# A two-layer encoder trunk on eight cores: the FFN down projection by seven block products, with residuals kept in DRAM

## The chip, the cores and the metric

The kernel runs on all 8 NeuronCores of one Trainium2 chip. Each core works on its own 2048 tokens; there is no traffic between cores. The metric is the device time of the slowest core, in microseconds (us). Cores 0 to 3 are one die, cores 4 to 7 the other.

Some executions of every version, the kernel before included, fall into a slower state: the cores of one die, sometimes of both, or a pair of cores, show a lower granted TensorE clock in the records, and the time is longer. Each such run is named below as slow or disturbed, and no difference is explained by one. Where a run of the kernel itself is compared, fast runs are compared with fast runs, and where single cores are compared, undisturbed cores with undisturbed cores.

## The reference, cut to what matters

```python
def swiglu(n, w_gate, w_up, w_down):
    return (jax.nn.silu(n @ w_gate) * (n @ w_up)) @ w_down

h = x                                   # (2, 8192, 1024) float32
for i in range(2):
    h = h + mixer_i(rms_norm(h))        # layer 0: convolutions, layer 1: chunked gating
    h = h + memory_cross_attention(rms_norm(h), mem)
    h = h + swiglu(rms_norm(h), w_gate[i], w_up[i], w_down[i])   # d_ff = 2816
return rms_norm(h)
```

## The kernel before

A core holds its tokens as four tiles of 512. `hT` is the float32 residual of the four tiles, kept in on-chip memory for the whole run (in the profile `hT_67` to `hT_70` are tiles 0 to 3); `nT` (`nT_71` to `nT_74`) is the normed input of a block in fp16. A Python scheduler lays out the five instruction streams ahead of time: it takes operations in program order, may look a few operations ahead on each engine (`AHEAD`), and picks by deadlines taken from its own cost model. So the order of each stream is fixed before the kernel runs, and an operation that waits holds back all that stands behind it in its stream.

Some words: a *slab* is a block of weights that one DMA loads; the *root* is the reciprocal root of a norm (`rs` in the traces), and the *scalings* multiply by it; a down phase without the seven products is called *plain*.

The FFN treats two token tiles at a time, a "pair"; the first pair is tiles 0 and 1, the second is tiles 2 and 3. It cuts d_ff into two runs of 12 and 10 blocks of 128. In each run there is a gate phase and then a down phase. The gate phase already uses seven block products instead of eight for a 2x2 block product (two feature blocks by two token tiles, with the contraction cut in two); the weight sums and input differences that this needs are made on VectorE. The down phase is plain:

```python
FPARTS = (12, 10)
AHEAD = {"pe": 6, "act": 32, "dve": 32, "pool": 1, "sp": 1}
...
for part, nf in enumerate(FPARTS):
    ...                                             # gate phase: seven products per unit
    for m in range(KC):                             # down phase: 8 output blocks
        w = self.wc(f"fd{part}", l, m)
        for ti, tt in enumerate(tts):
            rk = (lambda k, ti=ti: self.hid[ti][:, k, :])
            if part == 0:
                b = self.linear(w, nf, rk, self.hid_s[ti][0:nf], TT)
                # hT[tt][m] += ps[b]   (one addition on DVE)
                continue
            self.out_block(w, m, tt, nf, rk, self.hid_s[ti][0:nf], jobs[ti], 1)
            if m == KC - 1:
                if final:
                    self.push_store(tt, jobs[ti])
                else:
                    self.push_finish(jobs[ti], 5)
```

In the last layer the final norm works in place on `hT`, and the result is stored from there. This is pushed onto a queue of side work that is issued little by little while matmuls run:

```python
def push_store(self, tt, j, c0=0, n=TT, hs=None):
    def pair(k):
        j.scale(k)                                  # DVE: hT[k] *= gain * rstd, in place
        j.scale(k + 1)
        self.P.dma("sp", nm, hs[k:k + 2], (), out=self.out[tt, :, k:k + 2, c0:c0 + n],
                   in_=self.hT[tt][:, k:k + 2, c0:c0 + n])
    self.push(j.key, j.rstd, 5)
    for k in range(0, KC, 2):
        self.push(j.key, lambda k=k: pair(k), 5)
```

The start loads the input tiles one after the other behind the first weight slabs:

```python
self.load_x(0, "a", (), ("act", "sp"))
sl = [self.slab("ev_in", 0, c)[1] for c in (0, 4, 8, 16)]
self.load_x(1, "a", [sl[1]])                        # tile 1 behind the second weight slab
self.load_x(2, "a", [self.hT_s[1][4]])
self.load_x(3, "a", [self.hT_s[2][4]])
```

The softmax here doesn't subtract the row's maximum and nothing guards it: scores larger than these inputs give would overflow.

Of the kernel before, what the change touches and what calls it, by code (L numbers as in the profile page):

```python
# [14 lines left out]
KC = 8  # L15
# [9 lines left out]
FMAX = max(FPARTS)  # L25
KH = KC // 2
# [65 lines left out]
class Prog:  # L92
    ENGS = ("pe", "act", "dve", "pool", "sp")
    AHEAD = {"pe": 6, "act": 32, "dve": 32, "pool": 1, "sp": 1}
# [5 lines left out]
    DMA_RATE = 320e3  # L100
    EPOCH = 500
# [16 lines left out]
    def dma_part(self, eng, sem, slot, first, reads=(), **kw):  # L118
        prev = slot.w
        o = self.add(eng, lambda e: e.dma_start(**kw), reads, [slot] if first else [], dma=sem, cost=kw["in_"].nbytes())  # L120
        if not first:
            assert prev.dma == sem
            slot.w = o
        return o
# [47 lines left out]
    def schedule(self):  # L172
# [4 lines left out]
        link = 0.0  # L177
# [128 lines left out]
WCOLS = {"fgu": 512, "od_v": 512, "xo": 512}  # L306
# [9 lines left out]
class Builder:  # L316
    def __init__(self):
# [11 lines left out]
        self.wcache = {}  # L329
        self._declare_dram()  # L330
# [34 lines left out]
    def _declare_dram(self):  # L365
        nc = self.nc

        def din(name, shape):
# [9 lines left out]
                  for n, L, K, C in WSHAPES}  # L378
        self.out = nc.dram_tensor("out", [NT, 128, KC, TT], F32, kind="ExternalOutput").ap()

    def _alloc(self):
# [92 lines left out]
        sw_lo = tw_lo - 3 * KH * 2 * 128 * 2  # L474
        self.off = sw_lo
        self.sw, self.sw_s = self.tiles("sw", [128, 3, KH, 2, 128], FP16, 3)
        self.off = sw_lo - 2 * FMAX * TT * 2
        self.hid, self.hid_s = [], []
        for t in range(2):
            a, b = self.tiles(f"hid{t}", [128, FMAX, TT], FP16, FMAX)  # L480
            self.hid.append(a)
            self.hid_s.append(b)
        self.off = self.ends["ff"] = sw_lo - 2 * FMAX * TT * 2 - 6 * TT * 4
# [147 lines left out]
    def ld(self, name, layer, c0, at=None, after=()):  # L631
# [10 lines left out]
        self.wn += 1  # L642
        flat = self.nc.alloc_sbuf_tensor_at(f"wbuf{i}", [128, kc * cw], FP16, offset=lo)
# [5 lines left out]
        return flat[:, :].rearrange("p (k c) -> p k c", c=cw), sl  # L649

# [99 lines left out]
    def first_norms(self):  # L750
        js = [self.main_job(t, V_GMIX, pre=False, split=True) for t in range(NT)]
# [4 lines left out]
        for j, lag in ((js[0], 0), (js[1], 4), (jh, 8), (js[2], 10), (js[3], 18)):  # L756
# [42 lines left out]
    def l0_mixer(self):  # L799
# [19 lines left out]
        order = [(0, TT), (1, TT), (-1, H2), (2, TT), (3, TT)]  # L819
# [3 lines left out]
        def by_chunk():  # L823
# [3 lines left out]
            for q in range(2):  # L827
                for k in range(KC):
                    def fn(e, k=k, q=q):
                        for b, w in list(zip(bs, ws))[2 * q:2 * q + 2]:  # L830
                            ins = e.matmul(self.ps[b][:, :], lhsT=w[0](k), rhs=self.nT[0][:, k, :], start=(k == 0),
                                           stop=(k == KC - 1))
                        return ins
                    P.add("pe", fn, reads=[ws[2 * q][1][0], self.nT_s[0][k]],
                          writes=[self.ps_s[b] for b in bs[2 * q:2 * q + 2]], cost=2 * _mm_cost(TT))
                    self.tick(0.25)
            for b in bs:
                self.reserved.discard(b)
            first.update(zip(cs, bs))

        def side_a(tt, n, j):
            rk, rs = rhs_of(tt)
            if tt == 0 and j < 2:
                bv, bg = first[j], first[4 + j]
# [51 lines left out]
        def gated(tt, half):  # L896
            if tt in (2, 3):
                gate_b(tt - 1, half)
            elif tt < 0:
                gate_b(0, half)  # L900
        rhs_of(0)
        by_chunk()
        for tt, n in order:
            for j in range(2):
# [128 lines left out]
    def l1_mixer(self):  # L1033
# [10 lines left out]
        for fh in range(2):  # L1044
            self.slab("od_v", 0, 4 * fh, self.kv_lo if fh else None)
# [99 lines left out]
    def xattn(self, l):  # L1145
# [40 lines left out]
        def out(tt, m):  # L1186
            self.out_block(((lambda k: self.VW[:, k, m * 128:(m + 1) * 128]), self.VW_s), m, tt, KC,
                           lambda k: pt(tt, k)[0], [pt(tt, k)[1] for k in range(8)], jobs[tt], 3)
            if m == KC - 1:
# [42 lines left out]
    def weight_sums(self, slab, ss, s21):  # L1232
        w = slab.rearrange("p k (g j c) -> p k g j c", g=2, j=2)
        a11, a12, a21, a22 = w[:, 0:KH, :, 0, :], w[:, KH:KC, :, 0, :], w[:, 0:KH, :, 1, :], w[:, KH:KC, :, 1, :]
# [4 lines left out]
        return [lambda: tt(t[:, 0], a21, a22, ALU.add, ts[0], [ss, s21]),  # L1239
# [325 lines left out]
```

## Time and profile before

| | before |
|---|---|
| time, median of 3 runs | 1618.05 us (1617.05 to 1618.2) |
| spans of the eight cores, profiled run | 1608.9 to 1616.7 us |
| TensorE (PE) busy | 1581.7 us, 98% |
| VectorE (DVE) busy | 1035.0 us, 64% |
| moved by DMA | 130.66 MB |

This is the head of the profile page of the kernel before, with the row of TensorE from its 40-slice table (a digit is the busy share of a slice in tenths) and its chain of waits, by engine:

```profile
PE 1581.7 (98%) x7930; PEld 759.5 (47%) x7930; DVE 1035.0 (64%) x1662; ACT 710.0 (44%) x1174; POOL 71.5 (4%) x150
...
PE   6999999999999999999999999999999999999998
...
PE 94%; DMA 3%; ACT 1%; issue 1%; DVE 1%; POOL 0%; DVEq 0%; ACTq 0%; POOLq 0%; SPq 0%
```

The kernel is bound by TensorE everywhere but in the first slice and at the very end. The chain of work that ended last, near the end of the kernel, shows a down phase of run 0, with the plain start of the gate phase behind it, as one piece of 208 matmuls (start, length, what):

```profile
1469.89 44.89 PE ps L624 x208
```

That is 215.8 ns for a matmul of 512 columns. The Trainium skill, "TensorE: Matmul & The Clock Gate", § Back-to-back issue gap, gives N/2.4 + 2.5 ns warm, which is 215.8 ns for N = 512; here the trace agrees to the digit (that section calls it the gap of an isolated matmul; see the last section). So a **loss** can be computed for any stage of the kernel: its length less the sum of N/2.4 + 2.5 ns over its matmuls. The stage ledger in this document was made that way, from the matmul records of the trace. Its stages run from the first matmul of one to the first of the next.

These are three stretches of core 5, the slowest one before: the two kinds of down phase, then the last layer's first gate phase of the second pair. The columns are busy us of the engines with the number of instructions, the granted clock, the busy share of the 16 DMA engines, and GB/s:

```profile
508.50:549.90 41.40, 41.40 (x193) 18.74 (x192) 14.17 (x22) 0.63 (x1) 1.06 (x2) 1.00 0.37 70
611.10:645.60 34.50, 34.50 (x161) 15.68 (x160) 22.70 (x39) 10.07 (x16) 0.68 (x2) 1.00 0.43 81
1395.90:1469.70 73.80, 73.49 (x341) 33.19 (x340) 55.35 (x85) 47.68 (x72) 4.23 (x8) 1.00 0.68 147
```

On core 5, the slowest one before, a down phase of run 0 (508.50 to 549.90 us) is 192 matmuls in 41.40 us, one of run 1 (611.10 to 645.60 us) 160 in 34.50 us, with PE busy all the time. The gate phase has 340 matmuls in 73.80 us, while DVE is busy 55 of the 74 us.

### The profile page before, as it was taken

What the parts mean: (1) busy time and instruction counts of PE and PEld (TensorE: products, weight loads), DVE (VectorE), ACT (ScalarE), POOL (GpSimd) and SP (SyncE); (2) the same over time, 40 slices, a digit from 0 to 9 for tenths busy, and PEclk for the clock granted to TensorE, in tenths of its full rate; (3) what the DMA queues carried; (4) which work ended last, traced back from release to release, by engine and by line L of the source; (5) the groups of instructions that cost most, each with busy time, mean ns of one, the idle gap of its engine ahead of it and who ended that gap; (6) DMA issues with size and microseconds to landing.
All of it is one profiled execution on the core that took longest, in us unless ns stands there. A gap on an engine that the chain in (4) does not pass through costs nothing.

```text
span 1616.7 us, 24172 instructions; the slowest of 8 cores (1608.9 to 1616.7 us)
## 1 busy us (share of the span) xinstructions
PE 1581.7 (98%) x7930; PEld 759.5 (47%) x7930; DVE 1035.0 (64%) x1662; ACT 710.0 (44%) x1174; POOL 71.5 (4%) x150
## 2 busy tenths in 40 slices
PE   6999999999999999999999999999999999999998
PEld 2444674444444444444444455544444444444445
DVE  3777575656895466773656864755788357684456
ACT  2523475455462143740536533455555134371243
POOL 1000010000000000000000000000000000000000
PEclk9999999999999999999999999999999999999999
DMA  8344269310245263453453155130065344475342
GB/s 197 86 92 80 40 108 220 79 27 1 53 79 95 48 110 74 92 92 73 75 96 64 27 80 91 21 58 1 0 110 105 72 78 92 79 155 118 69 90 105
DMA packets 31193, 130.66 MB, mean 81 GB/s; under 512 B 3680, under 2 KB 8160, under 8 KB 24544
## 3 DMA queue, kind: packets, MB, share of 16 engines
q0 software_dynamic: 18720, 100.03, 35.1%
q1 hardware_dynamic: 12064, 28.04, 5.8%
q8 instruction: 67, 1.10, 0.3%
q10 hardware_dynamic: 288, 1.05, 0.2%
q14 instruction: 54, 0.44, 0.1%
HBM read 216.51 MB, written 8.39 MB: 139 GB/s over the span
## 4 chain that ended last, share of the span: by engine, by line
PE 94%; DMA 3%; ACT 1%; issue 1%; DVE 1%; POOL 0%; DVEq 0%; ACTq 0%; POOLq 0%; SPq 0%
PE ps L624 66%; PE ps L622 23%; PE ps L110 2%; PE ps L783 1%; PE ps L1137 1%; DMA wbuf_113<-w_ev_in 1%; DMA hT_68<-x_in 1%; DMA wbuf_131<-w_ev_out 0%; PE ps L1082 0%; DMA wbuf_192<-w_od_out 0%; DMA wbuf_199<-w_xqT 0%; ACT yst L110 0%; ACT L110 0%; ACT t_3_66 L110 0%; DVE pT L110 0%
## 5 line engine op out<-in xcount | busy, mean ns | idle before, releaser
L110 ACT ACTIVATE ps<-ps 128x512 f32<-128x512 f32 x88 | 50.9, 581 | 198.2 <-PE ps L624 197.7
L624 PE MATMUL ps<-pT,VW 128*128 128x512 f16 x512 | 118.7, 379 | 2.5 <-DVE pT L110 2.5
L110 DVE TENSOR_TENSOR hT_67<-hT_67,ps 128x512 f32<-128x512 f32 x64 | 44.0, 687 | 69.1 <-PE ps L624 66.7
L622 PE MATMUL ps<-tw,sw 128*128 128x512 f16 x352 | 83.5, 379 | 0.0
L624 PE MATMUL ps<-tw,sw 128*128 128x512 f16 x352 | 83.3, 379 | 0.0
L624 PEld LDWEIGHTS ps<-pT,VW 128*128 128x128 f16 x512 | 49.9, 98 | 63.4 <-issue 3.4
L110 ACT ACT_TABLE_LOAD x50 | 64.2, 1283 | 32.4 <-DMA hT_67<-x_in 9.3
L110 DVE TENSOR_TENSOR hT_68<-hT_68,ps 128x512 f32<-128x512 f32 x64 | 43.9, 686 | 47.0 <-PE ps L624 46.9
L110 DVE TENSOR_TENSOR hT_69<-hT_69,ps 128x512 f32<-128x512 f32 x64 | 43.9, 686 | 46.4 <-PE ps L624 46.1
L110 DVE TENSOR_TENSOR hT_70<-hT_70,ps 128x512 f32<-128x512 f32 (+1 forms) x72 | 44.9, 627 | 43.4 <-PE ps L624 39.2
L110 ACT ACTIVATE pT<-ps,epsc 128x512 f16<-128x512 f32 x64 | 43.7, 683 | 27.0 <-PE ps L624 25.8
L624 PEld LDWEIGHTS ps<-tw,sw 128*128 128x128 f16 x352 | 34.5, 98 | 41.5
L622 PEld LDWEIGHTS ps<-tw,sw 128*128 128x128 f16 x352 | 34.5, 98 | 41.5
L110 ACT ACTIVATE t_2_65<-ps 128x512 f32<-128x512 f32 (+1 forms) x53 | 30.8, 581 | 48.9 <-PE ps L624 33.0
L110 ACT ACTIVATE t_0_63<-ps 128x512 f32<-128x512 f32 (+1 forms) x56 | 32.2, 574 | 35.8 <-PE ps L624 23.2
L622 PE MATMUL ps<-nT_72,sw 128*128 128x512 f16 x176 | 41.6, 379 | 0.6 <-DVE w_4_105 L110 0.6
L622 PE MATMUL ps<-nT_74,sw 128*128 128x512 f16 x176 | 41.9, 379 | 0.0
L110 DVE TENSOR_TENSOR w_2_103<-ps,w_2_103 128x512 f32<-128x512 f32 x29 | 20.0, 691 | 27.9 <-ACT w_2_103 L110 15.3
L110 DVE SCALAR_TENSOR_TENSOR nT_72<-hT_68,vec,rs_62 128x512 f16<-128x512 f32 x48 | 33.7, 746 | 4.1 <-ACT rs_62 L110 4.1
L624 PE MATMUL ps<-X,wd 128*128 128x256 f16 x288 | 35.9, 272 | 0.0
L110 DVE SCALAR_TENSOR_TENSOR nT_71<-hT_67,vec,rs_61 128x512 f16<-128x512 f32 x48 | 34.4, 747 | 2.3 <-ACT rs_61 L110 2.3
L110 ACT ACTIVATE t_1_64<-ps 128x512 f32<-128x512 f32 (+1 forms) x42 | 24.2, 577 | 25.0 <-PE ps L624 16.4
(1292 smaller groups left out, 3391.1 us busy)
## 6 DMA issues: line engine op xcount, KB each, us to landing
hT_68<-x_in SPq DMA_DIRECT2D x8, 512.0 KB, 12.1
hT_69<-x_in SPq DMA_DIRECT2D x8, 512.0 KB, 7.2
hT_70<-x_in SPq DMA_DIRECT2D x8, 512.0 KB, 10.2
X<-a_ph SPq DMA_DIRECT2D x16, 130.0 KB, 2.8
out<-hT_67 SPq DMA_DIRECT2D x4, 512.0 KB, 7.0
out<-hT_68 SPq DMA_DIRECT2D x4, 512.0 KB, 6.7
out<-hT_69 SPq DMA_DIRECT2D x4, 512.0 KB, 3.3
out<-hT_70 SPq DMA_DIRECT2D x8, 256.0 KB, 2.2
```

The lines of the kernel that those rows point to most:

```text
L110: o = self.add(eng, lambda e: getattr(e, meth)(**kw), reads, writes, cost=_op_cost(eng, kw))
L622: ins = e.matmul(out, lhsT=l, rhs=r, start=False, stop=(i == np_ - 1), skip_group_check=True)
L624: ins = e.matmul(out, lhsT=l, rhs=r, start=(i == 0), stop=(i == np_ - 1))
L783: ins = e.matmul(self.ps[b][:, i * NMEM:(i + 1) * NMEM], lhsT=ws[i][0](k), rhs=mn[:, k, :], start=(k == 0), stop=(k == KC - 1))
L1137: ins = e.matmul(self.ps[b][:, i * NMEM:(i + 1) * NMEM], lhsT=w(c), rhs=self.kT[:, c, :], start=(hc == 0), stop=(hc == 1))
```

## The change

The change has three parts.

1. **The down projection too goes by seven block products.** 32 matmuls for two token tiles and a pair of d_ff blocks become 28. It needs differences of hidden tiles (`ht`) and weight sums, made on DVE, and more residual additions.
2. **The residual of the pair that is not being worked on is kept in DRAM** (`h_kept`), to make room; a load of it back is called a *recall*. Of each token tile and half, the hidden blocks 0 to 3 lie in memory of their own; the blocks 4 and 5 ("far", `hidf`) and the differences (`ht`) lie in the residual memory of the other pair. For the second pair this is `hT` of tiles 0 and 1. The scheduler's look-ahead on the sync queue, which issues the stores and recalls, goes from 1 to 8.
3. **At the start**, tile 1 is loaded after the first weight slab, not the second; the norms of tiles 1 to 3 add up squares on DVE so that they need 2 matmuls, not 8; and tiles 1 and 2 run chunk by chunk behind their scaling, as tile 0 did.

The diff, cut to its core:

```diff
-    AHEAD = {"pe": 6, "act": 32, "dve": 32, "pool": 1, "sp": 1}
+    AHEAD = {"pe": 6, "act": 32, "dve": 32, "pool": 1, "sp": 8}
...
+        self.h_kept = nc.dram_tensor("h_kept", [NT, 128, KC, TT], F32, kind="Internal").ap()
...
+        for h in range(2):
+            self.off = self.hT_s[2 - 2 * h][0].rng[0]          # place: the other pair's residual
+            self.ht.append(self.tiles(f"ht{h}", [128, 3, FMAX // 2, TT], FP16, 3 * FMAX // 2))
+            self.hid.append([(near[t], self.tiles(f"hidf{h}{t}", [128, 2, far, TT], FP16, 2 * far)) for t in range(2)])
...
     def first_norms(self):
-        js = [self.main_job(t, V_GMIX, pre=False, split=True) for t in range(NT)]
+        js = [self.main_job(t, V_GMIX, pre=t > 0, split=True) for t in range(NT)]
...
+    def close():                                  # at the end of gate unit 3 and of the last one
+            for key in kb.spent if tts[0] else ():
+                kb.want(key)                       # issue the other pair's norm and stores first
+            sub(t(0), f(1, 0), f(0, 0))            # differences of hidden tiles, on DVE
+            sub(t(1), f(1, 1), t(0))
+            sub(f(1, 0), f(1, 1), f(1, 0))
+            sub(t(2), f(0, 1), t(1))
...
+            if h == 1 and 3 <= i < 6:              # second pair: fetch its own residual
+                for tt in tts:
+                    for k in ((0, 2), (4,), (6,))[i - 3]:
+                        self.recall(tt, k, [u.w[1]])
...
+    def keep(self, tt, k):
+        self.P.dma("sp", f"hk{tt}_{k}", self.hT_s[tt][k:k + 2], [self.hk_s[tt][k // 2]],
+                   out=self.h_kept[tt, :, k:k + 2, :], in_=self.hT[tt][:, k:k + 2, :])
+
+    def recall(self, tt, k, after=()):
+        self.P.dma("sp", f"hr{tt}_{k}", [self.hk_s[tt][k // 2]], self.hT_s[tt][k:k + 2], after,
+                   out=self.hT[tt][:, k:k + 2, :], in_=self.h_kept[tt, :, k:k + 2, :])
...
-        self.load_x(1, "a", [sl[1]])
+        self.load_x(1, "a", [sl[0]])
```

The last down phase (run 1 of the second pair in the last layer) stays plain.

## The prediction

> **What bounds the kernel now.** TensorE: PE is busy 98% of 1616.7 us (first table), and the chain that ended last is 94% PE. Warm matmuls take 216 ns each (chain: 44.89 us for 208). By stretches, the two down projections of a half (509–550, 612–646 us) are 100% busy. The losses are in the first 60 us: real work starts at 18.9 us, and the timeline shows 128x512 matmuls at 430 ns after idle gaps. The Trainium skill, "TensorE: Matmul & The Clock Gate", on the back-to-back issue gap, gives N/1.2 GHz cold and N/2.4 + 2.5 ns warm: 427 and 216 ns, as traced.
>
> **What the change removes.**
> 1. Down projection by seven products: a d_ff run with n pairs needs 28n matmuls for two token tiles instead of 32n. Run 0 (n=6): 192 to 168, four times; run 1 (n=5): 160 to 140, three times (the last stays plain). 156 x 216 ns = 33.7 us of PE, nearly all on the critical path.
> 2. First norms of tiles 1 to 3: squares pre-added on DVE, 2 matmuls instead of 8 each: 18 x 216 ns = 3.9 us.
> 3. Start: tile 1 is loaded after the first weight slab (landed 16.2 us) instead of the second (20.1 us), and tiles 1, 2 run chunk by chunk behind their scaling. Before, tile 1 begins at 47.2 us after a 2.4 us wait, with cold matmuls. I expect 4 to 5 us.
>
> **What it adds.** DVE, now 64% busy:
> - per 512-column unit 12 residual additions instead of 8 (687 ns each);
> - four weight sums: 690 ns at 1024 fp16 in the trace, estimated 960 and 830 ns at 1536 and 1280;
> - per run and token pair four differences of hidden tiles, estimated 1.2 us (2048 fp16) plus 0.4 to 0.7.
>
> Back to back, DVE operations start about 610 ns apart. Over one layer's FFN (434–857 us) DVE goes from 265 of 423 us to about 340 of 404. Tightest is run 0's gate phase of the second token pair (646–720 us before, 55.6 of 74 busy): it gets hidden differences and later norm work, about 72 of 72.5 us at the 610 ns spacing; and the far hidden tiles there must wait until the other pair's norm has read its residual. The first pair's run 1 down has 27 to 33 of 30 us. I expect PE stalls of 1 to 4 us each, some 6 us in all.
>
> DMA: 24 MB more for residuals, on 130.7 MB at 40% mean share. Slabs of 2 MB land in 8.5 us against 12 us per gate unit; the larger fd slabs in an estimated 10 to 13 against 15 to 18. Off the path.
>
> **Sum.** 1618 - 33.7 - 3.9 - 4.5 + 6 = 1582; I say 1583 us, range 1571 to 1597. This is close to the 2% line (1585.7): faster 0.6, same 0.38, slower 0.02.
>
> **What would show each step.** PE matmuls fall by about 174. A run 0 down phase takes 36.3 us instead of 41.4, run 1 30.2 instead of 34.5. PE's waits on DVE in the FFN (hidden tiles, differences, residual additions) in the list of waits show the part given back. Tile 1's first matmul comes at 38 to 40 us. DVE rises to 1180–1200 us busy, 75%. PE waits for no recalled tile.
>
> **What would make it wrong.** DVE falling behind in the gate phases, so that PE loses 10 us or more per layer: then 1595 or above. Final stores of the first pair landing too late for the hidden tiles that take their place. Slabs, recalls and stores colliding, so that weights arrive late. The start gaining nothing, since 8 MB must land by about 33 us either way. On the other side, no stalls and a start gain of 8 us give 1573.

## The result, and the profile after

| | before | after |
|---|---|---|
| fast runs, same rounds | 1617.05 to 1619.74 us (median of 4: 1618.12) | 1603.81, 1608.75, 1608.24 us |
| other runs | none | 1884.55 and 1873.84 us, slow |
| ratio of fast runs | 1 | 0.993 (0.9907 to 0.9953) |
| spans of the cores, profiled fast run | 1608.9 to 1616.7 us | 1582.9 to 1602.3 us |
| DVE busy | 1035.0 us, 64% | 1157.0 us, 72% |
| moved by DMA | 130.66 MB | 155.84 MB |

A ratio here is the mean time of one kernel's fast runs over that of the other's in the same rounds, with a 95% interval, so it is not quite the ratio of the medians that are quoted. The change makes the kernel 0.7% faster. That is inside the 2% band and outside the predicted range of 1571 to 1597 us.

The head of the page after, with the same rows:

```profile
PE 1547.1 (97%) x7756; PEld 742.1 (46%) x7756; DVE 1157.0 (72%) x1836; ACT 758.9 (47%) x1270; POOL 63.1 (4%) x134
...
PE   7899989999999999999999999999999999978998
...
PE 90%; DMA 6%; DVE 1%; issue 1%; ACT 1%; POOL 0%; SPq 0%; DVEq 0%; POOLq 0%; ACTq 0%
PE ps L634 52%; PE ps L632 32%; PE ps L112 2%; DMA out<-hT_67 2%; PE ps L808 1%; PE ps L856 1%; PE ps L1164 1%; DMA wbuf_137<-w_ev_out 1%; DMA hT_68<-x_in 1%; DMA wbuf_152<-w_fd 1%; DMA wbuf_118<-w_ev_in 1%; DMA hT_69<-x_in 1%; PE ps L1109 
```

The 174 matmuls are gone (7930 to 7756). But PE now has a 7 and an 8 in slices 36 and 37 (and an 8 in slices 2 and 6, the start and the mixer output of layer 0), and the chain holds 6% of DMA, with `DMA out<-hT_67` first: that is the first pair's final store, which nothing after it in the reference needs. The cores have come apart as well. This is the view of the cores of the kernel after, its first die (span, mean granted clock):

```profile
core 0: 1602.3 us, clock 0.987
core 1: 1586.2 us, clock 0.993
core 2: 1599.5 us, clock 0.990
core 3: 1582.9 us, clock 0.992
```

The other die is alike (1583.4, 1602.0, 1585.5 and 1597.7 us). In each pair of cores (0 and 1, 2 and 3, and so on) one is 12 to 19 us longer than its neighbour; before it was 3 to 6 us.

The stage ledger, slowest core against slowest core (core 5 before, core 0 after). The whole difference is 1602.3 - 1616.7 = -14.4 us:

| stage | before: length (loss) | after: length (loss) | difference |
|---|---|---|---|
| start and first projections | 179.9 (24.6) | 176.9 (25.6) | -3.0 |
| convolution | 54.5 (2.1) | 53.2 (0.8) | -1.2 |
| layer-0 mixer output | 72.7 (4.2) | 77.0 (8.5) | +4.3 |
| four run 0 down phases | 4 x 41.4 (0.0) | 38.0 (1.7), 3 x 36.3 (0.0) | -19.0 |
| three run 1 down phases | 3 x 34.5 (0.0) | 3 x 30.2 (0.0) | -12.9 |
| layer 0, gate phase, second pair, run 0 | 73.8 (0.5) | 74.9 (1.5) | +1.0 |
| **last layer, gate phase, second pair, run 0** | 73.8 (0.5) | **89.9 (16.5)** | **+16.0** |
| last layer, gate phase, second pair, run 1 | 60.4 (0.0) | 61.6 (1.2) | +1.2 |
| all the rest | | | -0.8 |

Here are the same kinds of stretch on core 0 after, as shown of before: the two kinds of down phase (the first row is run 1 of the first pair, the third is run 0 of the second pair in layer 0), and between and below them the second pair's first gate phase of layer 0 (second row) and of the last layer (fourth row):

```profile
608.00:638.20 30.20, 30.20 (x141) 13.70 (x140) 24.41 (x44) 10.71 (x18) 2.11 (x4) 1.00 0.57 116
638.20:713.10 74.90, 74.23 (x341) 32.79 (x340) 69.36 (x110) 52.71 (x83) 2.11 (x4) 1.00 0.87 193
713.10:749.40 36.30, 36.30 (x170) 16.46 (x169) 29.61 (x44) 7.10 (x12) 2.11 (x4) 1.00 0.41 75
1369.40:1459.30 89.90, 75.62 (x342) 33.14 (x341) 68.82 (x110) 50.03 (x80) 2.11 (x4) 0.92 0.75 170
```

The down phases are what was predicted, and PE is busy in every microsecond of them. The second and the fourth row are the reading that matters. Both phases do the same work: 110 instructions on DVE, 69 us of them, and both recall 4 MB. One loses 1.5 us and the other 16.5. So the load on DVE, which the prediction feared most, is not what costs the 15 us. In the last layer the final stores of the first pair read the memory that the far hidden tiles are to take. Layer 0 has stores there too, eight of 512 KB into `h_kept`, but they need no scaling and go out early. This is what the sync engine issued there (start, time to issue, what); the phase begins at 638.2 us:

```profile
621.01 1.28 SPq L117 DMA_DIRECT2D h_kept<-hT_67  x2
...
650.53 2.12 SPq L117 DMA_DIRECT2D h_kept<-hT_68  x2
659.62 0.81 SPq L117 DMA_DIRECT2D hT_70<-h_kept  x2
```

The stores of layer 0 were issued from 17 us before the phase to 14 us into it. They too were slow, up to 23 us to landing, in DMA traffic that was no lighter (193 GB/s over the phase, against 170). But the last had landed 31 us into the phase, and nothing waited for them. So the two layers differ in *when* the stores are issued, and not in their number or in the bytes moved.

The waits of core 0 in the last layer's phase (engine, what waits, what it waits for, us in total, times, longest):

```profile
PE ps L634 <- DVE hidf_105 L112: 14.1, 1, 14.1
...
DVE hidf_105 L112 <- DMA out<-hT_68: 11.0, 1, 11.0
...
DVE ht_104 L112 <- DMA out<-hT_67: 5.0, 1, 5.0
```

TensorE waits for a far hidden tile, and DVE, which is to write it, waits for the store that still reads that memory. On the four better cores (1, 3, 4 and 6) the profile names a gate tile on DVE instead (8.1 to 9.6 us), but DVE had stood still for the same stores there, on core 3 for 5.2 and 4.7 us. The chain says the same in order of time (start, length, what):

```profile
1414.98 30.52 DMA out<-hT_67
...
1446.73 0.70 DVE hidf_105 L112
...
1447.57 3.24 PE ps L634 x8
1450.80 8.63 PE ps L632 x40
```

A store of 512 KB took 30.5 us. The eight matmuls after the wait took 3.24 us, 405 ns each, where the 40 behind them took 216 ns each. The Trainium skill, "TensorE: Matmul & The Clock Gate", § HAM oscillation, says that a TensorE idle for more than about 3.4 us falls back to half its clock; the trace agrees for this wait of 14.1 us (405 ns is near double of 216, and the mean clock of the phase is 0.92, in the window row above). It does not test the 3.4 us; e5 below bears on them. So the 16.5 us are 14.1 us of waiting and about 1.5 us of cold matmuls, (405 - 216) ns x 8, and little else.

Why 30.5 us? This is what the sync engine issued in that stretch (start, time to issue, what):

```profile
1403.50 0.34 SPq L117 DMA_DIRECT2D out<-hT_68  x1
1404.08 1.06 SPq L117 DMA_DIRECT2D hT_69<-h_kept  x2
1405.35 1.27 SPq L117 DMA_DIRECT2D hT_70<-h_kept  x2
...
1411.51 0.84 SPq L117 DMA_DIRECT2D out<-hT_68  x1
1414.98 7.96 SPq L117 DMA_DIRECT2D out<-hT_67  x2
```

One store goes out, then all eight recalls (4 MB), and the other stores behind them, as DVE finishes the scalings. The phase began at 1369.4 us, so the first store was issued 34 us into it and the next five at 42 to 58 us; 12 of the 16 scalings run 33 to 58 us into it. (The last two stores came at 81 and 114 us; no matmul of this phase waited for them.) The stores issued at 42, 45.6, 53.2, 57 and 58.3 us landed at 70.4, 76.1, 77.3, 78.6 and 79.8 us. Two weight slabs of 1.5 MB for the coming down phase were issued at 49 and 61 us on the other queue. In the 45.7 us from the first store on, the 16 DMA engines were busy to 92% and moved 231 GB/s:

```profile
1403.50:1449.20 45.70, 31.63 (x143) 13.99 (x142) 27.91 (x43) 15.98 (x28) 1.05 (x2) 0.86 0.92 231
```

The Trainium skill, "DMA: Bandwidth & Descriptors", § Issuing engines are not separate DMA queues, says that transfers started from different engines run on the same 16 DMA engines and interleave. The trace agrees: stores, recalls and slabs, from two issuers, landed late together.

So there are two candidate reasons for the late landing: the stores are **issued late** (the scalings stand late in DVE's order), and they **share the DMA engines** with the recalls and slabs. The experiments take them apart.

### The profile page after: what moved, and what is told of

Read it like the earlier page. It is cut to its first block, busy times and chain, and to the rows that moved or that the text cites. A ratio compares the mean times of both kernels' runs of the same rounds, so it can differ in the third digit from the quotient of the medians.

```text
span 1602.3 us, 24520 instructions; the slowest of 8 cores (1582.9 to 1602.3 us)
## 1 busy us (share of the span) xinstructions
PE 1547.1 (97%) x7756; PEld 742.1 (46%) x7756; DVE 1157.0 (72%) x1836; ACT 758.9 (47%) x1270; POOL 63.1 (4%) x134
## 2 busy tenths in 40 slices
DMA packets 35804, 155.84 MB, mean 97 GB/s; under 512 B 4192, under 2 KB 8672, under 8 KB 27104
## 4 chain that ended last, share of the span: by engine, by line
PE 90%; DMA 6%; DVE 1%; issue 1%; ACT 1%; POOL 0%; SPq 0%; DVEq 0%; POOLq 0%; ACTq 0%
PE ps L634 52%; PE ps L632 32%; PE ps L112 2%; DMA out<-hT_67 2%; PE ps L808 1%; PE ps L856 1%; PE ps L1164 1%; DMA wbuf_137<-w_ev_out 1%; DMA hT_68<-x_in 1%; DMA wbuf_152<-w_fd 1%; DMA wbuf_118<-w_ev_in 1%; DMA hT_69<-x_in 1%; PE ps L1109 0%; DMA wbuf_197<-w_xqT 0%; ACT t_3_66 L112 0%
## 5 line engine op out<-in xcount | busy, mean ns | idle before, releaser
L112 ACT ACTIVATE ps<-ps 128x512 f32<-128x512 f32 x116 | 67.3, 581 | 111.3 <-PE ps L634 111.0
L634 PE MATMUL ps<-tw,sw 128*128 128x512 f16 x352 | 84.5, 384 | 14.1 <-DVE hidf_105 L112 14.1
L112 ACT ACT_TABLE_LOAD x50 | 64.2, 1283 | 36.6 <-DVE small L112 9.6
L634 PEld LDWEIGHTS ps<-tw,sw 128*128 128x128 f16 x352 | 34.5, 99 | 57.1 <-issue 17.2
L112 ACT ACTIVATE t_2_65<-ps 128x512 f32<-128x512 f32 (+1 forms) x54 | 31.4, 582 | 49.8 <-PE ps L634 32.3
L112 ACT ACTIVATE w_0_107<-ps 128x512 f32<-128x512 f32 x39 | 23.3, 596 | 59.6 <-PE ps L632 57.2
L112 ACT ACTIVATE w_4_111<-ps 128x512 f32<-128x512 f32 x38 | 22.6, 595 | 46.7 <-PE ps L632 46.7
L112 ACT ACTIVATE w_2_109<-ps 128x512 f32<-128x512 f32 x39 | 23.2, 596 | 42.0 <-PE ps L632 36.8
L112 ACT ACTIVATE t_1_64<-ps 128x512 f32<-128x512 f32 (+1 forms) x43 | 25.2, 586 | 24.6 <-PE ps L634 14.1
L112 DVE SCALAR_TENSOR_TENSOR nT_73<-hT_69,vec,rs_61 128x512 f16<-128x512 f32 x48 | 34.0, 746 | 3.3 <-ACT rs_61 L112 3.3
```

Of the source, the lines that this page charges most:

```text
L112: o = self.add(eng, lambda e: getattr(e, meth)(**kw), reads, writes, cost=_op_cost(eng, kw))
L634: ins = e.matmul(out, lhsT=l, rhs=r, start=(i == 0), stop=(i == np_ - 1))
```

## The experiments

Seventeen runs were made, of fifteen kernels (e16 and e17 repeat e13 and e14), in five calls, each call on one chip with its own runs of the kernel before. Losses below are those of the last layer's first gate phase of the second pair, called *the phase*, on the eight cores of the profiled execution, from its first matmul to the first of the next down phase, unless another stage is named. The names of tiles in these traces have no numbers (`hT`, `out<-hT`).

| run | edit, on the kernel after | fast runs, us | ratio to before | loss of the phase, us |
|---|---|---|---|---|
| (after) | | 1603.81 to 1608.75 | 0.993 | 11.5 to 17.6 |
| e1_recall_early | recall at units 0 to 2 | 1590.19 to 1597.0 | 0.9862 | 0.9 to 1.8 on five cores, 11.1 to 11.5 on three |
| e2_no_recall | no recall in the last layer (wrong result) | 1594.41, one run | | 0.9 to 2.5 on five, 7.2 to 9.2 on three |
| e3_sp_in_order | sync look-ahead 1 | 1604.18 to 1606.46 | 0.9931 | 8.9 to 15.7 |
| e4_start_before | the old start | 1605.87, 1606.66 | unclear | 10.3 to 17.0 |
| e5_norm_sooner | norm and stores much sooner | 1598.34 to 1599.21 | 0.9892 | 11.0 to 12.8 |
| e6_early_sooner | e1 and e5 | 1597.7 to 1598.88 | 0.989 | 11.0 to 12.6 |
| e7_root_first | tile 1's root before tile 2's squares | 1597.25 to 1599.9 | 0.9888 | 12.3 to 15.8 |
| e8_all_three | e1, e5 and e7 | 1593.9 to 1597.21 | 0.9869 | 11.0 to 12.6 |
| e9_lead40 | e1 and norm moderately sooner | 1591.2 to 1594.2 | before disturbed | 3.2 to 3.4 |
| e10_reload_late | a reload in layer 0 later | 1602.13 to 1605.88 | before disturbed | 11.9 to 17.8 |
| e11_four, e12_three | combinations | disturbed | inconclusive | 3.2 to 3.4; 0.7 to 10.3 |
| e13, e14, e15 | combinations | chip throttled | none | not used |
| e16_again | e1, norm moderately sooner, e7 | 1585.96 to 1589.08 | 0.9815 | 3.2 to 3.4 |
| e17_oldstart_again | e16 with the old start | 1594.22 to 1596.64 | 0.987 | 3.2 to 3.4 |

### First call: what delays the stores, and the start

**e1_recall_early.** The recall of the last layer goes to gate units 0 to 2, ahead of the final norm, so that the 4 MB are out of the way when the stores come.

```diff
-            if h == 1 and 3 <= i < 6:
+            r0 = 0 if final else 3
+            if h == 1 and r0 <= i < r0 + 3:
                 for tt in tts:
-                    for k in ((0, 2), (4,), (6,))[i - 3]:
+                    for k in ((0, 2), (4,), (6,))[i - r0]:
```

> Edit: in the last layer alone, the kept residual of the second token pair is fetched back in gate units 0 to 2 of its FFN instead of 3 to 5, so the 4 MB stand ahead of all the first pair's output stores and not between the first and the seven others. In the changed kernel the gate phase of that pair (run 0, last layer) lost 11.5 to 17.6 us on the 8 cores beyond the ideal matmul time, against 0.5 to 0.9 before. Theory A (the fetch, queued ahead of seven of eight stores, delays their landing, and the far hidden tiles wait for it): the loss falls to 2 to 6 us and the slowest core to 1588 to 1594 us. Theory B (VectorE is so full in this phase that the final scalings, which the stores wait for, come too late by themselves): the loss stays above 9 us and the time above 1598 us.

Measured: fast runs 1597.0, 1590.19 and 1594.96 us, ratio 0.9862 (0.9835 to 0.9889). One further run was slow, at 1767 us. The phase lost 0.9 us on cores 1, 3, 5 and 6, 1.8 us on core 7, and 11.1 to 11.5 us on cores 0, 2 and 4. On core 1 TensorE waited for nothing in the phase: its three stores issued at 53, 57 and 58 us landed at 61.7, 62.9 and 65.1 us. On core 0 the stores issued at the same moments landed at 64.9, 66.9 and 76.3 us, and this is what DVE waited for there:

```profile
DVE ht L112 <- DMA out<-hT: 6.5, 1, 6.5
DVE hidf L112 <- DMA out<-hT: 3.3, 1, 3.3
```

So each of the two theories of the expectation holds on some cores. Removing the recall from in front of the stores is worth the whole loss on some and part of it on others. The stores are still issued late, and then some 10 us of DMA traffic decide.

**e2_no_recall.** The recall of the last layer is taken away and the memory is cleared on GpSimd instead. This gives a wrong result (relative error 0.82): it only measures the wait without the 4 MB.

```diff
-                        self.recall(tt, k, [u.w[1]])
+                        if final:
+                            self.P.op("pool", "memset", (), self.hT_s[tt][k:k + 2], ap=self.hT[tt][:, k:k + 2, :], constant=0.0)
+                        else:
+                            self.recall(tt, k, [u.w[1]])
```

> Edit: the last layer does not fetch the second pair's residual back; GpSimd sets its place to zero instead, so the result is wrong on purpose. This bounds what the fetch can cost. Theory A (fetch delays stores): the loss of the phase falls to 1 to 5 us, stores land 4 to 10 us after issue. Theory B (VectorE scalings late): the loss stays at 8 us or more with no fetch at all.

Measured: 1594.41 us. The phase lost 0.9 to 2.5 us on five cores and still 7.2 to 9.2 us on cores 1, 3 and 6. So the recall is not the only cause: with it gone altogether, stores that are issued at 53 to 58 us still land too late on some cores, at up to 75 us. The weight slabs are in flight at that time, but no run moved them, so their part is not shown.

**e3_sp_in_order.** The look-ahead of the sync queue goes back to 1, so recalls can't pass stores.

```diff
-    AHEAD = {"pe": 6, "act": 32, "dve": 32, "pool": 1, "sp": 8}
+    AHEAD = {"pe": 6, "act": 32, "dve": 32, "pool": 1, "sp": 1}
```

> Edit: one number, the look-ahead of the scheduler for the sync queue back from 8 to 1, as before the change. DMAs are then issued in program order: all eight stores of the first pair, then the fetch. Theory A: the loss of the last layer's gate phase falls to 3 to 8 us (the fetch now comes late, a new wait of 0 to 4 us may appear where the residual is added), slowest core 1588 to 1596 us. Theory B: loss stays above 9 us. Also, the ev_out stage, where on three cores the changed kernel lost 6.4 to 8.5 us waiting for weights behind the reloads of x issued 8 us earlier than before, should go back to 3 to 4 us if the earlier reload is the cause; if it is chance of the shared memory, it stays.

Measured: fast runs 1604.18 to 1606.46 us, ratio 0.9931 (0.9914 to 0.9948), one slow run of 1631 us. The loss of the phase was 8.9 to 15.7 us, against 11.5 to 17.6 with the look-ahead. Even this overstates the gain: here 20 of the 340 matmuls of the phase are issued after the next down phase has begun. Over the same work (this phase, the down phase and the next gate phase, 788 matmuls) e3 lost 12.3 to 18.2 us and the kernel after 12.7 to 18.8, so nothing was gained. The theory that the order in the queue alone is at fault had expected a loss of 3 to 8 us and missed. The recalls now do stand behind all the stores, but the queue waits for each scaling in turn: on core 0 the stores were issued at 45, 53, 58 and 66 to 68 us and landed as late as 83 us.

**e4_start_before.** The start is as it was before the change; everything else is new.

```diff
-        js = [self.main_job(t, V_GMIX, pre=t > 0, split=True) for t in range(NT)]
+        js = [self.main_job(t, V_GMIX, pre=False, split=True) for t in range(NT)]
...
-        self.load_x(1, "a", [sl[0]])
+        self.load_x(1, "a", [sl[1]])
...                      # the order of tiles, chunk-by-chunk work and loads as before
```

> Edit: the start as before the change (order of loads, first norms, order of ev_in tiles, only tile 0 chunk by chunk); all else as changed. Prediction of record: the new start is worth 8 us. Theory C (the new start gains little, because tile 1 still lands at 31 to 33 us, and its reciprocal root stands on ScalarE behind the squares of tile 2, at 41.5 to 46.3 us against 37.6 to 41.0 before): the start stage takes 175 to 180 us against 172 to 177, and the time is 0 to 4 us above the changed kernel's. Rival (the start is worth 8 us and was eaten elsewhere): 7 to 10 us slower than the changed kernel.

Measured: 1605.87 and 1606.66 us in the undisturbed runs; two others, at 1627 us, had cores 2 and 3 at a clock of 0.975. The ratio over all, 0.9981 (0.9888 to 1.0073), is unclear for that reason. The start took 175.5 to 177.2 us on all eight cores. In the kernel after it took 172.4 to 174.2 us on one core of each pair and 176.5 to 176.9 us on the other. So the new start gives up to 4 us on the better core of a pair and nothing on the worse one, which sets the time. The convolution stage was back to 54.3 to 54.6 us, where the new start has 53.2: its 1.2 us belong to the new start.

### Second call: sooner stores, and the root

**e5_norm_sooner.** The final norm is pushed ahead in the static order: the scheduler is told that a final store takes 80 us, and the side work is issued at double rate, so scalings and stores come in the first half of the phase.

```diff
-                lead = o.cost + self.LAT[o.eng] if o.dma is None else 2.0 + o.cost / self.DMA_RATE
+                lead = o.cost + self.LAT[o.eng] if o.dma is None else (80.0 if o.dma[0] == "o" else 2.0) + o.cost / self.DMA_RATE
...
-            self.tick_n = 1
+            self.tick_n = 2 if final and (i < 3 if h else todo[min(i + 1, len(todo) - 1)][0] == "fd1") else 1
```

> Edit: all as changed, but the scheduler takes the output stores to need 80 us of lead instead of 2, and two queued norm steps instead of one go out per tick around that place, so the 16 final scalings of the first pair stand some 30 VectorE instructions earlier; the fetch of the other residual is issued between the stores. In the run with the early fetch one core of each pair of neighbours was healed (loss 0.9 us, from 11.5 to 17.6) and the other not (11 us): there the last stores were issued 53 to 58 us into the phase and landed at 65 to 76 us, behind a 3 MB weight slab. Theory D (late scalings and the fetch in front are one fault: stores issued too late for the far hidden tiles at 59 us): with scalings at 25 to 45 us all 8 cores lose under 4 us in the phase; slowest core 1586 to 1593 us. Rival (on the slower core of a pair the DMAs are just too slow, whenever issued): it still loses 7 us or more. Rival B2 (VectorE has no room, so scalings moved up delay the gate work): new PE waits on hidden tiles of 4 us or more earlier in the phase.

Measured: fast runs 1598.34 to 1599.21 us, ratio 0.9892 (0.9873 to 0.9911); a fourth run was slow. On core 0 all eight stores were issued by 43 us and had landed by 50 us. No write of a hidden tile waited for a store any more. Yet the phase lost 11.0 to 12.8 us, now on every core alike. These are the waits of TensorE in it on core 0, and two lines of DVE's timeline:

```profile
PE ps L634 <- ACT t L112: 2.8, 1, 2.8
PE ps L112 <- DVE sqp L112: 2.6, 1, 2.6
PE ps L632 <- DVE sw L112: 1.4, 1, 1.4
PE ps L632 <- ACT ps L112: 0.9, 2, 0.7
```

```profile
1380.41 5.39 DVE L112 SCALAR_TENSOR_TENSOR hT<-hT,vec,rs 128x512 f32<-128x512 f32 x8 [1.69 <-ACT rs L112]
...
1390.03 4.07 DVE L112 SCALAR_TENSOR_TENSOR hT<-hT,vec,rs 128x512 f32<-128x512 f32 x6 [0.21 <-ACT rs L112]
```

The scalings now go first whenever they can: eight of them in a row for 5.4 us, six for 4.1 us, after an idle stretch of DVE for the root. The gate work that TensorE needs next stands behind them (the second and third wait). The first wait is one for ScalarE: the root, with a load of its function table before it and another after it, takes ScalarE from 1377.6 to 1382.1 us, and the gate activation that TensorE needs comes next. So the wait moved: from the stores to the order of DVE and ScalarE. Some 2 us of the loss are cold matmuls: after two gaps of 3.0 and 2.8 us with 0.9 us of matmuls between them, matmuls started 427 ns apart, though neither gap reaches the 3.4 us named above. This run takes the waits for stores away, without moving the recall, and keeps a loss, so it also says that the final norm must not be pushed this far.

**e6_early_sooner.** e1 and e5 together, with the two edits shown.

> Edit: early fetch and early scalings together. Theory D: loss of the phase 0.5 to 2 us on all 8 cores, slowest core 1583 to 1590 us, against 1590 to 1597 for the early fetch alone and 1604 to 1609 as changed. If the slower core of each pair still loses 7 us or more, its cause is neither.

Measured: fast runs 1597.7 to 1598.88 us, ratio 0.989 (0.9872 to 0.9907), one run slow. The phase lost 11.0 to 12.6 us on every core, as in e5. With the stores early the place of the recall has no effect, which agrees with e5's reading that the order of the engines sets this loss.

**e7_root_first.** Only the start: tile 2's squares on ScalarE may not be placed before tile 1's reciprocal root.

```diff
-            P.op("act", "activation", [src_s[k]], [q.slot], out=q.t[:, 0:n], in_=src_k(k), func=AF.Square)
+            o = P.op("act", "activation", [src_s[k]], [q.slot], out=q.t[:, 0:n], in_=src_k(k), func=AF.Square)
+            if j.behind is not None:
+                o.after.append(j.behind.root)
...
+            j.root = st["r"].slot.w          # in rstd()
...
+        js[2].behind = js[1]                 # in first_norms()
```

The reason lies in the trace of the kernel after. ScalarE on core 0 (start, length, what, idle before): tile 1 (`hT_68`) is squared by 33.8 us, but the root of its norm (`rs_62`) comes at 46.3 us, behind all of tile 2's squares (`hT_69`), which wait for tile 2's load:

```profile
33.19 0.63 ACT L112 ACTIVATE sq_58<-hT_68 128x512 f32<-128x512 f32 x1
...
38.91 0.63 ACT L112 ACTIVATE sqa_59<-hT_69 128x512 f32<-128x512 f32 x1 [2.70 <-DMA hT_69<-x_in]
...
46.28 0.63 ACT L112 ACTIVATE rs_62<-t_3_66 128x512 f32<-128x512 f32 x1
```

> Edit: all as changed, but tile 2's squares at the start must follow tile 1's reciprocal root on ScalarE. As changed, tile 1 has landed at 31.3 to 32.8 us and its root stands at 41.5 to 46.3 us. Theory C (the instruction order on ScalarE, made for loads that land earlier than they do, holds back tile 1): root at 36 to 39 us, tile 1's first matmul at 38 to 41 us instead of 43.3 to 48.0, the start stage 3 to 5 us shorter (168 to 174 us instead of 172.4 to 176.9), time 3 to 5 us below the changed kernel's 1604 to 1609. Rival (the start is bound by the loads of tiles 2 and 3): tile 1 is earlier, the stage within 1.5 us of as changed.

Measured: fast runs 1597.25 to 1599.9 us, ratio 0.9888 (0.9869 to 0.9908). The root of tile 1 came at 37.1 to 38.7 us (41.5 to 46.3 in the kernel after). The start took 169.1 to 172.5 us. In the mean this is 3.8 us less than in the kernel after on the better core of a pair, and 4.5 us less on the worse one, as expected. The loss of the phase stayed at 12.3 to 15.8 us, as it should.

**e8_all_three.** e1, e5 and e7 together, expected to add up.

> Edit: early fetch, early scalings and root first together: the candidate to beat both. By the sum of the parts: 1618 less 33.7 (products) less 8 (start, with the root first) plus 2 to 6 (waits for weights on the slower core of each pair) is 1579 to 1586 us, ratio 0.977 to 0.982 to before.

Measured: fast runs 1593.9 to 1597.21 us, ratio 0.9869 (0.985 to 0.9888), one run slow. The start was 169.0 to 172.3 us, but the phase lost 11.0 to 12.6 us, since e5's edit is in it. The expectation of 1579 to 1586 us was missed, for the reason that e5 had shown.

### Third call: a moderate lead, and a reload in layer 0

**e9_lead40.** e1, and e5 with a lead of 40 us in place of 80.

```diff
-                ... else 2.0 + o.cost / self.DMA_RATE
+                ... else (40.0 if o.dma[0] == "o" else 2.0) + o.cost / self.DMA_RATE
```

> Edit: the early fetch, with a lead of 40 us for stores instead of 80. With 80 no store was waited for any more (last one landed at 48 to 50 us into the phase), yet every core lost 11.0 to 12.8 us: eight and six final scalings stood in one block on VectorE (5.4 and 4.1 us) and TensorE waited for the gate work behind them. With 40 they stand in groups of two to four, at about 22 to 48 us. Theory E (what counts is both: scalings early enough for the stores and spread enough for the gate work): the loss of the phase is 1 to 4 us on all 8 cores, slowest core 1584 to 1591 us. Rival (VectorE has no room for earlier scalings at all): loss again 8 us or more on every core, also on those that the early fetch alone had healed to 0.9 us.

Measured: 1591.2 to 1594.2 us in four runs. The runs of the kernel before on this chip were disturbed (median 1637.98 us, a pair of cores at a lower clock; the undisturbed ones 1616.8 to 1617.3), so the ratio of 0.9782 (0.9666 to 0.9897) is not used. The phase lost 3.2 to 3.4 us **on all eight cores**. These are the waits of TensorE in it on core 0:

```profile
PE ps L632 <- DVE tw L112: 1.1, 1, 1.1
PE ps L632 <- DVE w L112: 0.8, 1, 0.8
PE ps L112 <- DVE sqp L112: 0.6, 2, 0.3
```

Seven of the eight stores were issued at 20 to 44 us and had landed by 49 us (the eighth, at 95 us, was not waited for); the first difference was written at 59.1 us and waited for nothing. DVE does the same work as in the kernel after (69.6 us busy in the phase), and what remains are waits of about 1 us. This is what shows the cause: with the same instructions on DVE and the same bytes, and only the order changed, 11.5 to 17.6 us become 3.3. (A lead of 40 us without e1's earlier recall was not run, so whether e9 needs that half is not shown.)

**e10_reload_late.** Another stage had lost time that was not predicted: the output projection of the layer-0 mixer lost 6.4 to 8.5 us on cores 0, 2 and 5 of the kernel after (3.1 to 4.2 before). On core 0 TensorE waited 5.5 us for a 512 KB weight slab that took 13.7 us to land; on its neighbour core 1 the same slab took 6.6 us and was not waited for. The guess was that the reload of input tile 1, issued at that time, delays it. The edit moves the reload behind those slabs.

```diff
-                if i == 3:                    # reload after the last silu
+                if i == 3 and nh:
...
+            if tt == 0:
+                self.load_x(1, "b", [self.yA_s[0]] + [self.slab("ev_out", 0, c)[1] for c in (0, 2, 4, 6)])
```

> Edit: all as changed, but the reload of x tile 1 (2 MB) waits until all four ev_out weight slabs have landed. As changed it is issued at 226 to 227 us, just before three of the slabs, and on the slower core of a pair ev_out loses 6.4 to 9.0 us, against 3.1 to 4.2 before. Theory F (the reload is in the way of the slabs): loss 2 to 5 us on all cores, time 2 to 4 us below as changed. Rival (the slower core of a pair has slow DMAs whatever the order): loss stays above 6 us on four cores.

Measured: 1602.13 to 1605.88 us (the runs of before are those of e9). The wait for the slab fell from 5.5 to 0.6 us, but new waits came, for the reloaded tile and for another transfer. The stage still lost 7.2 to 9.1 us on the worse core of each pair. The guess is not borne out: the wait moved and the stage did not get shorter.

**e11_four** (e9, e7, e10) and **e12_three** (e1, e7, e10) were to show the sum.

> Edit: early fetch, lead 40, root first and late reload together. If theories C, E and F hold: 1576 to 1584 us, ratio 0.975 to 0.980. If E fails, 1588 to 1594 us.

> Edit: early fetch, root first and late reload, with no change of lead: what the safe parts give. One core of each pair at 1565 to 1570 us, the other still waiting for stores, 7 to 11 us in the last gate phase: slowest core 1580 to 1590 us, ratio 0.977 to 0.983.

Measured: medians 1619.32 and 1622.0 us, with two to six cores at a clock near 0.977 in every run; these lost some 24 us more in the start stage than the undisturbed cores of the same execution. The ratios, 0.9938 (0.982 to 1.0057) and 0.9962 (0.9866 to 1.0057), say nothing about the kernels. The undisturbed cores were at 1587.3 us or less in the profiled run of e11. Both are inconclusive.

### Fourth and fifth call: the best version

Three kernels were sent to a chip that turned out to be throttled throughout (clock 0.90 to 0.93 on all cores, lower still in some runs; the kernel before took 1767 us there): e13 is e1, the 40 us lead and e7; e14 is the same with the old start; e15 has a lead of 30 us.

> Edit: early fetch, lead of 40 us for the stores, root of tile 1 first. Sum of what the parts showed: last gate phase loses 3.2 us on all cores, start 169 to 173 us; slowest core 1584 to 1589 us, ratio 0.979 to 0.984 to before on an undisturbed chip.

> Edit: early fetch and lead of 40 us, but the start as before the change. If the new start makes the two cores of a pair differ and the later one lose in ev_out, then here the pair's spans lie within 6 us, ev_out loses 3 to 6 us, and the slowest core is at 1590 to 1595 us. If the start has nothing to do with it, one core of each pair still loses 7 us or more in ev_out.

> Edit: as e13_early40_root with a lead of 30 us. If the 3.2 us of the last gate phase are gate work behind blocks of scalings, the loss falls to 1 to 2.5 us on the quicker cores; if the scalings then come too late for the stores on the slower core of a pair, it loses 4 us or more there. Time within 3 us of e13_early40_root.

Measured: 1726.43, 1727.28 and 1725.38 us in the median.

**e16_again** is e13's file.

> The kernel of e13_early40_root once more, for an undisturbed chip. As there: last gate phase loses 3.2 us on all cores, start 169 to 173 us, slowest core 1584 to 1589 us, ratio 0.979 to 0.984 to before.

Measured: fast runs 1589.08, 1587.1 and 1585.96 us against 1614.86 to 1617.57 us of before; ratio 0.9815 (0.9796 to 0.9833), the smallest of all that are usable. Other runs were slow: two at about 1616 us with one pair of cores at 0.972 to 0.979, one of 1648 us, and one of 1893 us with a die at 0.81. The phase lost 3.2 to 3.4 us on all cores, and the start took 169.2 to 172.9 us. This is the view of its cores:

```profile
core 0: 1585.3 us, clock 0.996
core 1: 1572.8 us, clock 0.995
core 2: 1586.4 us, clock 0.996
core 3: 1574.6 us, clock 0.995
```

and the like on the other die. This version beats both kernels: about 1587 us, against 1604 to 1609 and 1618.

**e17_oldstart_again** is e14's file: the old start with everything else of e16.

> The kernel of e14_early40_oldstart once more. If the new start makes the two cores of a pair differ and the later one lose in ev_out: the pair's spans within 6 us, ev_out loses 3 to 6 us, slowest core 1590 to 1595 us. If not: one core of each pair still loses 7 us or more in ev_out.

Measured: fast runs 1595.52, 1594.22 and 1596.64 us, ratio 0.987 (0.9854 to 0.9885), the fourth slow. So the new start, with the root first, is worth some 8 us against the old one: 4 to 5 us in the start stage on the worse core of a pair, which sets the time (177.2 to 177.3 us on the undisturbed ones here, against 172.0 to 172.9), and 1.2 us or a little more in the convolution, which sum to some 6; the rest is not traced. The cores of a pair are still 10 to 12 us apart with the old start, so the new start is not what splits them.

## Why the prediction was wrong

**The matmuls and the down phases: right.** 174 matmuls fewer were predicted and measured, and 36.3 and 30.2 us for the down phases. This gave 33.7 us on every core, less 1.8 us where a weight slab came late in the first one.

**DVE in general: right in sign, too dark.** DVE rose to 1157 us (72%), below the 1180 to 1200 predicted. The same load of 69 us in 74 cost 1.5 us in layer 0. "DVE falling behind in the gate phases" did not happen.

**The step that failed: "I expect PE stalls of 1 to 4 us each, some 6 us in all", with the DMA "Off the path."** In the last layer's gate phase of the second pair the stall was 11.5 to 17.6 us. The prediction had named this phase as the tightest and had noted that "the far hidden tiles there must wait until the other pair's norm has read its residual". It did not follow that sentence one step on: after the norm a *store* reads the same memory, so the tile waits for the landing of a DMA, not for DVE. In layer 0 that store needs no scaling, and the last one had landed 31 us into the phase; in the last layer the norm works in place and the store can only follow it. It listed "Final stores of the first pair landing too late" among the dangers, and gave it no size. The runs size it: six of the eight stores were issued 34 to 58 us into the phase, because the scalings stand that late in DVE's order, and then shared the DMA engines with 4 MB of recall and 3 MB of slabs, up to 30 us to landing. The space is needed from about 59 us on. Each half of this cause was taken away by itself. Without the recall in front (e1, e2) the loss vanished on five of eight cores and stayed at 7 to 11.5 us on the others. With sooner stores but a too greedy order on DVE (e5) no store was waited for, wherever the recall stood (e6), and 11 us were lost in another place. With both, in measure (e9), 3.3 us remained on all cores. So early stores are enough to end the waits for them; the recall out of the way is enough only on some cores. The sync look-ahead of 8, which put the recalls in front of the stores, is not the cause by itself (e3).

**The start: the term was mis-sized.** The prediction took 3.9 us for 18 matmuls and "4 to 5 us" for the earlier load. "Tile 1's first matmul comes at 38 to 40 us" was measured as 48.0 us on core 0 (44.1 on core 1), no sooner than the 47.2 us before. By the ledger the stage is 3.0 us shorter: the work of the 18 matmuls is gone (3.9 us), but the loss did not fall by the 4 to 5 us of the earlier load, it rose by 1.0 (24.6 to 25.6). Tile 1 was issued 3.5 us sooner (16.7 us on core 0, 20.2 on core 5 before) and its last part landed 2.0 us sooner (32.3 against 34.3), so part of that lead was lost on the way; the prediction had named this danger. The rest was lost after landing, and this was overlooked: the static order of ScalarE holds the root of tile 1 behind tile 2's squares. With the root first (e7) the start fell to 172.2 to 172.5 us on the worse core of a pair: against the 178 to 179.9 us of the slower cores before, some 6 to 8 us of the 8.4 predicted are then there.

**What was not predicted at all.** The layer-0 mixer output lost 4.3 us more on the slowest core, and other small waits for slabs appeared there. They sit on one core of each pair, which one varies from run to run: in every undisturbed execution of a changed kernel one core of each pair was 6 to 27 us longer than the other, mostly 10 to 20; in the undisturbed ones of the kernel before it was at most 6.2. The Trainium skill, "HBM Reference", § Specifications (TRN2), says that the two cores of a domain share its bandwidth. It would fit that the changed kernels, which move 19% more bytes, show more of it, but no run here tested it by leaving one core of a pair idle. Why one core of a pair loses throughout stays open. So does the mixer output: e10 removed the wait that the profile named and not the loss.

**The sum.** On the slowest cores the prediction had -33.7 - 8.4 + 6 = -36.1 us, and the ledger says -14.4. The gap of 21.7 us is: 12.9 us of stalls in the gate phases of the FFN (16.0 + 1.2 + 1.0 of the ledger and 0.7 in layer 0's first gate phase are 18.9, against 6), 5.4 us at the start, 4.3 us in the mixer output, 1.8 us for one late slab in a down phase, less 2.7 us of small gains in the convolution and elsewhere. The two parts whose causes were found, put right in e16, bring the time to about 1587 us, within 4 us of the prediction. That nearness is partly luck and confirms no term: e16 holds an edit that the prediction did not have (the root first) and the losses on one core of each pair that it did not foresee.

## What to carry to other kernels

When a buffer takes the place of another, ask what reads the old contents *last*, and when that can start; if it is a DMA store, its landing is the deadline, and the whole line in front of it counts: the operation that makes the data, the queue, and all else that the DMA engines move in that stretch. A safe order has to be found in measure: stores too late cost 11 to 18 us here, stores forced too early 11 to 13 us on VectorE and ScalarE, and the middle 3 us. And a load that lands sooner gained nothing here until the operation between it and its first use, in the static order of ScalarE, had moved as well.

## What the Trainium skill lacked or had wrong

- "TensorE: Matmul & The Clock Gate", § Back-to-back issue gap, calls N/2.4 + 2.5 ns the gap of an isolated matmul and gives about 131 ns for each in a sustained stream of N = 512. Here 208 matmuls of 512 columns in a row, with their weight loads, took 44.89 us, 215.8 ns each. The "isolated" formula was the sustained rate in every stage without loss, and no stage was faster. (An earlier passage of the page itself measures 215.7 ns back to back, so it is this section that is off.)
- The same page, § Seeing it yourself, says to budget 13/16 of the clock for dense matmuls on all cores. In the fast state all eight cores ran at a mean clock of 0.986 to 0.998 over the whole kernel, with TensorE 97 to 98% busy. The 13/16 does appear, in some executions (0.811 to 0.814 on one die in e16's run of 1893 us). So here it was a state that a run falls into and not the rule.
- No page has the state in which a pair of cores, at times two or three pairs, runs at a mean clock of 0.972 to 0.979, with some 24 us lost in one stretch, mostly the start (195.7 to 203 us against 169 to 177.5; in e4 some 26 us over the last three stages), while the other cores are undisturbed; nor a chip on which all cores stay at 0.90 to 0.93.
- "HBM Reference" and "DMA: Bandwidth & Descriptors", § Bandwidth, give about 358 GB/s for a core whose neighbour streams too. With stores, recalls and weight slabs mixed, the 16 DMA engines were busy to 92% at 231 GB/s (kernel after, 45.7 us of core 0). They give no figure for such mixed traffic, in which one store of 512 KB took 30.5 us.
- "HBM Reference" says that the cores of a pair share bandwidth, but no page says what the runs show, whether or not the sharing is the reason: one core of each pair ended 6 to 27 us later in every undisturbed execution of the changed kernels (10 to 14 us in those of e16 and e17, where the last layer's loss is the same on all cores).
- "ScalarE: Activation LUTs", § What ACT_TABLE_LOAD costs, counts about 1380 ns of drain on top of a load of 1283 ns. The load is 1283 ns here as well, but the next activation starts 1.29 us after the load did (33.84 to 35.13 us, core 0 of the kernel after), so no drain is seen.
